# Expert weights in 2 MB blocks with 16 KB rows, buffered in eight blocks of four slots, and another order of expert units

## The chip, the cores and the metric

The kernel runs on one core of one Trainium2 chip. Its engines are TensorE (PE, with its weight loads shown as PEld), VectorE (DVE), ScalarE (ACT), GpSimd (POOL) and SyncE (SP), whose queue issues nearly all loads from HBM. Each engine takes its own instructions in order and waits on semaphores for the others. The metric is the device time of one execution in microseconds, the median of several runs. All data are 32-bit floats.

## What is computed

Two layers over 256 latent tokens and 256 context tokens of width 1024. A layer modulates and normalises its input, mixes it with three head groups (a chunked gating MLP, a 2-D Fourier mixing, a windowed attention), projects, and applies a channel mixer. The channel mixer of layer 0 is dense; that of layer 1 sends each of the 256 latent tokens to two of eight experts of inner width 3584:

```python
logits = (y @ w_r).astype(jnp.float32) + b_r.astype(jnp.float32)
top_val, top_idx = lax.top_k(logits, TOP_K)
gates = jax.nn.softmax(top_val, axis=-1)
combine = jnp.sum(jax.nn.one_hot(top_idx, N_EXPERTS, dtype=jnp.float32) * gates[..., None], axis=-2)
for e in range(N_EXPERTS):
    out = out + combine[..., e:e + 1] * ((jax.nn.silu(y @ wg[e]) * (y @ wu[e])) @ wd[e])
```

Gate, up and down matrices of the eight experts are 352 MB together; every one of them is read once, whatever the routing.

## The kernel before

**An order written out beforehand.** The program is built by a planner (`Sched`, L91 on). Work is written as Python generators, called tasks; each step of a task names an engine, the buffers it needs and the events it waits for. The planner keeps a virtual clock for each engine, charges each instruction a cost (`Eng.cost`, L239; `DM` for a load of 512 KB in the expert stage), and always takes the step that could start first, with a bias per task. What comes out is one fixed instruction order for each engine. A buffer that a task takes in the plan becomes, on the chip, a wait for the readers of whatever was in it before.

**Buffers.** SBUF holds 41 slots of [128, 1024] floats (512 KB each, pool "s", `slot` L292), and smaller ones ("h", "q"). `get` (L133) gives out the slot that has been free longest. A load takes a slot in the class "raw"; `sc.rest` is the number of slots that loads must leave to all other uses (`avail`, L111). In the expert stage it is 8, from step 7 of the list below 17, and from step 28 again 8 (`REST`, L53): loads can fill 33, 24 and 33 slots.

**The expert stage.** `experts` (L1488) works through units. Unit None is expert 0, whose address is known from the start, with 32 token slots. Units 0 to 6 are the other seven experts by falling number of tokens, with 160, 96, 96, 64, 64, 64 and 32 token slots (`SLOTS`); SP reads their numbers into registers once the routing tables are made (`t_comb`, L1251, spawned with the bias `CB`; it ends with the table of overflowing tokens). What exceeds the slots of a unit is done in extra rounds under a branch (`moe_over`, L1646). `SEQ` (L68) lists the order as (unit, first block, last block): inner width 3584 is seven blocks of 512 columns, and one block of one unit is a step, 56 steps in all. Each entry of `SEQ` ends with a down product over its blocks and a finish (`t_finish`, `t_xfinish`), which spreads the result over the tokens and adds it up.

A step needs a gate, an up and a down piece of 2 MB, each loaded as four DMAs of 512 KB whose rows are 4 KB (`moe_items` L1674, `t_load` L378). The load order is gate and up of step n, then down of step n-1. Parts of 128 token slots (only unit 0 has one, beside a part of 32) use weights split into a high and a low half, made by ScalarE and VectorE (`t_hi` L401, `t_lo` L409), and three matmuls a product (`t_egu`, `t_edown`). Parts of 64 and 32 slots (`t_xgu` L1551, `t_xdown` L1592) read the loaded pieces as they are. `raw_done` (L418) and `done` (L423) free a slot after its last use, each 512 KB for itself. Within an entry of `SEQ` the gate and up tasks of all steps are spawned before the down task, so that in the plan they come first when both could run.

Of the kernel before, what the change touches and what calls it, by code (L numbers as in the profile page):

```python
# [24 lines left out]
D = 1024  # L25
KC = 8
NE = 8
# [32 lines left out]
LAT = (0.26, 0.2)  # L60
DF, DM = 0.4, 1.27
SGB, FOB, PRB = (-0.3, -0.3), (-0.3, -0.5), (-0.5, 0.0)
# [4 lines left out]

SEQ = ((None, 0, 7), (0, 0, 2), (3, 0, 7), (0, 2, 4), (4, 0, 7), (0, 4, 7), (5, 0, 7), (1, 0, 7), (2, 0, 7), (6, 0, 7))  # L68

# [21 lines left out]
class Sched:  # L91
# [3 lines left out]
    def __init__(self, make):  # L95
        self.make = make
        self.clock = {e: 0.0 for e in (PE, ACT, DVE, POOL, DMA, NONE)}
        self.live, self.cur, self.num = [], None, 0
        self.free, self.cap, self.held, self.own = {}, {}, {}, {}
        self.rest = 0  # L100

# [9 lines left out]
    def avail(self, res):  # L111

        need, cls_need = {}, {}
        for r in res:
            p, _, c = self.parse(r)
            need[p] = need.get(p, 0) + 1
            cls_need[p, c] = cls_need.get((p, c), 0) + 1
        t = 0.0
        for p, n in need.items():
            if len(self.free[p]) < n:  # L120
                return None
            t = max(t, self.free[p][n - 1][0])
        for (p, c), n in cls_need.items():
            if (p, c) in self.cap and self.held.get((p, c), 0) + n > self.cap[p, c]:
                return None
            if c == "raw" and len(self.free[p]) - n < self.rest - self.others():
                return None
        return t

    def others(self):  # L130
        return sum(n for (p, c), n in self.held.items() if p == "s" and c != "raw")

    def get(self, res):  # L133
        out = []
        for r in res:
            p, dt, c = self.parse(r)
            _, tag = self.free[p].pop(0)
# [44 lines left out]
    def step(self, t):  # L182
        self.live.remove(t)
        self.cur = t
        eng, res, _ = t.req
        if res:
            t.ready = max(t.ready, self.avail(res))
        try:
# [97 lines left out]
class Core:  # L286
# [5 lines left out]
    def slot(self, tag, dt=F32):  # L292
        return self.sb.tile([128, 1024], dt, tag=tag, name=tag)

# [83 lines left out]
    def t_load(self, items):  # L378
        for kind, key, ap in items:
            if kind == "rest":  # L380
                self.sc.rest = ap
                self.sc.cap["s", "raw"] = 40 if ap else 6
# [7 lines left out]
            if callable(ap):  # L390
                if self.uidx is None:
                    yield on(DMA, ev=[self.combed])
                    self.uidx = [self.nc.values_load(self.unum[0:1, r:r + 1], engines=(mybir.EngineType.SP,),
                                                     min_val=0, max_val=NE - 1) for r in range(NE - 1)]
                ap = ap()
            raw = yield on(DMA, "s:raw")
            self.nc.sync.dma_start(raw, ap)
            self.sc.charge(DMA, self.dcost)
            self.sc.set(self.raw[key], raw, 1.9)

    def t_hi(self, items):  # L401
        for kind, key, ap in items:
            if kind not in ("w", "wn"):
# [14 lines left out]
    def raw_done(self, key):  # L418
        self.ruses[key] -= 1
        if self.ruses[key] == 0:  # L420
            self.sc.rel(self.raw[key].v)

    def done(self, key):  # L423

        self.uses[key] -= 1
        if self.uses[key] == 0:
            self.sc.rel(*self.piece[key].v)

    def stream(self, items):

        items = [it if len(it) == 4 else (*it, 1) for it in items]
        for kind, key, ap, n in items:
            self.raw[key], self.piece[key], self.uses[key] = Event(), Event(), n
            self.ruses[key] = len(kind)
# [1053 lines left out]
    def experts(self, units, seq):  # L1488
# [3 lines left out]
        for key, b0, b1 in seq:  # L1492
# [27 lines left out]
            near = [hts[max(b0, b1 - 2)]]  # L1520
            if (key, b0, b1) == seq[-1] and key < NE:
# [124 lines left out]
    def moe_over(self):  # L1646

        tc, nc = self.tc, self.nc
        novf = nc.values_load(self.onum[0:1, MORE:MORE + 1], min_val=0, max_val=MORE)
        oidx = [nc.values_load(self.onum[0:1, i:i + 1], engines=(mybir.EngineType.SP,), min_val=0, max_val=NE - 1)  # L1650
# [23 lines left out]
    def moe_items(self, seq, idx=None):  # L1674
# [3 lines left out]

        def piece(name, e, *at):
            if idx is None and e == 0:  # L1680
                return a[name][(e, *at)]

            def by_register():
                i = self.uidx[e - 1] if idx is None else idx
                return a[name][(bass.ds(i, 1), *at)].rearrange("o p f -> (o p) f")

            return by_register

        kind = lambda e: "".join(dict.fromkeys("n" if ws else "w" for _, ws in self.parts(self.slots(e)))) if idx is None else "w"
        it = []  # L1690
        for n in range(len(steps) + 1):
            if n < len(steps):
                e, b = steps[n]
                if idx is None:
                    it += [("rest", None, r) for m, r in REST[1] if n == m]
                for k, name in (("eg", "w_gate_e"), ("eu", "w_up_e")):
                    it += [(kind(e), (k, e, b, j), piece(name, e, b, j)) for j in range(4)]
            if n > 0:
                e, b = steps[n - 1]
                it += [(kind(e), ("ed", e, b, j), piece("w_down_e", e, 4 * b + j)) for j in range(4)]  # L1700
        return it
# [42 lines left out]
    def build(self):  # L1744
        with self.tc.tile_pool(name="sb", bufs=1) as sb, \
                self.tc.tile_pool(name="ps", bufs=1, space=bass.MemoryType.PSUM) as psp:
            self.sb, self.psp = sb, psp
            with self.tc.manual_schedule():
                self.body()

    def body(self):
        nc, a = self.nc, self.a
        sc = self.sc = Sched({"s": self.slot, "h": self.half, "q": self.quarter, "b": self.bank, "p": lambda tag, dt: tag})
        sc.pool("b", [f"b{i}" for i in range(8)])
        sc.pool("s", [f"s{i}" for i in range(NS)])
        sc.pool("h", [f"f{i}" for i in range(NH)])
# [7 lines left out]
        R2, R8 = range(2), range(8)  # L1764
        self.raw, self.piece, self.uses, self.ruses, self.uidx = {}, {}, {}, {}, None
        self.gate, self.colev = ev(R2, (2, 5), R2), ev(R2, (0, 1, 3, 4, 5))
# [5 lines left out]
        self.hT = [Event() for _ in range(7)]  # L1772
        self.dcost = DM
        self.cev_h, self.lev_h, self.lev_c = [[Event() for _ in range(FC)] for _ in range(3)]
# [178 lines left out]
def _layout(i):  # L1953
# [51 lines left out]
```

## Time and profile before

| | us |
|---|---|
| median of 3 runs | 1710.16 (1707.85 to 1710.85) |
| the profiled execution, its own time | 1710.48 |
| its span, first to last instruction | 1708.6 |
| PE busy | 1635.1 (96%) |
| VectorE busy | 778.1 (46%) |
| ScalarE busy | 536.1 (31%) |
| moved by DMA | 497.78 MB, mean 291 GB/s |

The profile comes from one execution. Busy time is time with an instruction under way; PE's matmuls are pipelined and their ends are modelled. A matmul of plain 32-bit floats is two records, one on split halves is one. The granted clock is given as a share of full speed; its mean was 0.985. "Idle before" is the time in which the engine had nothing under way ahead of an instruction, with what ended it. Nearly all compute instructions carry line 232, the helper that records them, so groups are told apart by their shapes: `128*64 128x512` is a matmul with a stationary operand of 128x64 and an output of 512 columns.

### The profile page before, as it was taken

What the parts mean: (1) busy time and instruction counts of PE and PEld (TensorE: products, weight loads), DVE (VectorE), ACT (ScalarE), POOL (GpSimd) and SP (SyncE); (2) the same over time, 40 slices, a digit from 0 to 9 for tenths busy, and PEclk for the clock granted to TensorE, in tenths of its full rate; (3) what the DMA queues carried; (4) which work ended last, traced back from release to release, by engine and by line L of the source; (5) the groups of instructions that cost most, each with busy time, mean ns of one, the idle gap of its engine ahead of it and who ended that gap; (6) DMA issues with size and microseconds to landing.
All of it is one profiled execution on the core that took longest, in us unless ns stands there. A gap on an engine that the chain in (4) does not pass through costs nothing. (4 is left out here: it accounts for less than half of the span.)

```text
span 1708.6 us, 33100 instructions
## 1 busy us (share of the span) xinstructions
PE 1635.1 (96%) x13308; PEld 1146.5 (67%) x13308; DVE 778.1 (46%) x1426; ACT 536.1 (31%) x945; POOL 26.1 (2%) x49
## 2 busy tenths in 40 slices
PE   6999999999999999998987999999999999999995
PEld 3776889888888888886664754755675565466452
DVE  4576688765644458887506521620752110020022
ACT  3476453322222235556414312410531000000011
POOL 0100000000000010000000000000000000000000
PEclk9999999999999999999899999999999999999997
DMA  9515436544544455773699899999999999999995
GB/s 370 203 38 235 161 136 215 180 164 144 193 153 159 172 203 200 284 264 130 246 367 392 329 414 413 400 409 414 412 352 413 413 412 412 414 412 397 391 411 228
DMA packets 137890, 497.78 MB, mean 291 GB/s; under 512 B 16349, under 2 KB 16481, under 8 KB 137729
## 3 DMA queue, kind: packets, MB, share of 16 engines
q1 hardware_dynamic: 135072, 490.79, 74.9%
q0 software_dynamic: 1792, 4.18, 0.8%
q8 instruction: 106, 1.74, 0.4%
q10 hardware_dynamic: 864, 0.62, 0.1%
q14 instruction: 56, 0.45, 0.1%
HBM read 494.49 MB, written 1.05 MB: 290 GB/s over the span
## 5 line engine op out<-in xcount | busy, mean ns | idle before, releaser
L232 PE MATMUL b<-s,s 128*128 128x512 f32 (+3 forms) x6056 | 873.4, 344 | 18.7 <-DVE s L232 16.6
L232 PEld LDWEIGHTS b<-s,s 128*128 128x128 f32 (+2 forms) x6056 | 663.2, 157 | 192.2 <-issue 40.5
L232 PE MATMUL b<-s,f 128*32 128x128 f32 (+5 forms) x5472 | 520.6, 355 | 29.2 <-DVE ones L632 8.6
L232 PEld LDWEIGHTS b<-s,f 128*32 128x32 f32 (+2 forms) x5472 | 319.2, 129 | 206.1 <-issue 92.8
L232 DVE TENSOR_TENSOR s<-s,s 128x1024 fp32r<-128x1024 f32 (+2 forms) x253 | 303.1, 1216 | 70.4 <-ACT s L232 60.3
L232 ACT ACTIVATE s<-s 128x1024 fp32r<-128x1024 f32 (+1 forms) x257 | 265.4, 1052 | 180.5 <-PE b L232 94.2
L232 DVE TENSOR_TENSOR f<-f,b 128x256 f32<-128x256 f32 (+3 forms) x91 | 39.0, 430 | 469.5 <-PE b L232 469.3
L232 ACT ACTIVATE f<-b 128x512 f32<-128x512 f32 (+4 forms) x161 | 77.6, 483 | 425.8 <-PE b L232 424.8
L232 PE MATMUL b<-s,q 128*64 128x512 f32 (+2 forms) x752 | 161.0, 587 | 6.0 <-issue 4.5
L232 DVE SCALAR_TENSOR_TENSOR s<-s,cs,s 128x1024 f32<-128x1024 f32 x73 | 91.8, 1279 | 40.1 <-DMA s<-in_w_ada_dram 39.8
L232 ACT ACTIVATE q<-b 128x128 f32<-128x128 f32 (+2 forms) x53 | 18.0, 341 | 256.1 <-PE b L232 256.1
L232 PEld LDWEIGHTS b<-s,q 128*64 128x64 f32 (+2 forms) x752 | 47.5, 132 | 74.3 <-issue 53.4
L232 DVE TENSOR_TENSOR s<-b,s 128x512 fp32r<-128x512 f32 (+2 forms) x85 | 53.8, 638 | 80.0 <-ACT s L232 57.3
L232 ACT ACTIVATE s<-b 128x512 fp32r<-128x512 f32 (+3 forms) x107 | 54.6, 533 | 86.5 <-PE b L232 75.3
L232 PE MATMUL b<-ident,f 128*128 128x128 f32 x313 | 56.5, 290 | 7.0 <-DVE smx L232 3.1
L232 PEld LDWEIGHTS b<-ident,f 128*128 128x128 f32 x313 | 35.0, 143 | 41.8 <-DVE f L232 22.4
L232 DVE SCALAR_TENSOR_TENSOR s<-b,utab,s 128x512 f32<-128x512 f32 x56 | 40.8, 748 | 42.1 <-PE b L232 42.0
L232 ACT ACTIVATE f<-f 128x256 fp32r<-128x256 f32 x28 | 11.7, 419 | 114.9 <-DVE f L232 114.9
L232 PEld LDWEIGHTS b<-q,h 128*128 128x128 f32 x288 | 35.6, 200 | 5.7 <-issue 2.4
L232 DVE TENSOR_TENSOR f<-b,f 128x512 fp32r<-128x512 f32 x5 | 3.4, 689 | 78.5 <-ACT f L232 78.5
L232 PE MATMUL b<-q,h 128*128 128x32 f32 (+3 forms) x288 | 36.9, 284 | 0.8 <-DVE q L232 0.8
L232 ACT ACTIVATE f<-b,cols 128x256 f32<-128x256 f32 (+1 forms) x56 | 25.9, 555 | 34.4 <-PE b L232 31.3
(154 smaller groups left out, 565.9 us busy)
## 6 DMA issues: line engine op xcount, KB each, us to landing
s<-in_w_gate_e_dram SPq DMA_DIRECT2D x224, 512.0 KB, 10.0
s<-in_w_up_e_dram SPq DMA_DIRECT2D x224, 512.0 KB, 10.0
s<-in_w_down_e_dram SPq DMA_DIRECT2D x224, 512.0 KB, 10.0
s<-in_w_ada_dram SPq DMA_DIRECT2D x96, 512.0 KB, 4.5
s<-in_w_down_d_dram SPq DMA_DIRECT2D x56, 512.0 KB, 4.3
s<-in_w_gate_d_dram SPq DMA_DIRECT2D x28, 512.0 KB, 4.3
s<-in_w_up_d_dram SPq DMA_DIRECT2D x28, 512.0 KB, 3.4
s<-in_w_in_dram SPq DMA_DIRECT2D x24, 512.0 KB, 7.5
```

Source lines behind the costliest of these rows:

```text
L232: r = f(out, *a, **k)
```

## The change

The arrays of the expert weights are laid out so that one gate, up or down piece of a step is 128 rows of 16 KB, and one DMA loads all 2 MB. For that the last 32 of the 41 slots are made as eight small pools of four ("low"); the first nine (`KEEP`) stay single. `block` gives up such a pool and forms one tile of [128, 4096] in its place ("high", pool "Q") as soon as its four slots are free and a load asks for it. Until step 6 a load may also take four single slots, as four DMAs of 512 KB; then only blocks. From step 7 to 28, loads leave three blocks to the split halves, which now live in blocks too, two pieces in each. A block is freed when all four pieces in it are used. Single slots are no longer given out oldest first: among those free for 4 us (`SLACK`), the first nine go first, and then those of the group with the fewest free. The planner's cost of an expert load falls from 1.27 to 1.22 for 512 KB, the bias of the routing tables from 12.5 to 3.0, unit 6 is cut in two around unit 2, and the parts of a step are spawned in reverse, the 32-slot part of unit 0 first. Before the overflow rounds, all remaining groups become blocks.

```diff
-CB = 12.532
+CB = 3.0
-REST = (8, ((7, 17), (28, 8)))
+REST = (0, ((6, 9, 0), (7, 9, 3), (28, 9, 0)))
+KEEP, SLACK, NEAR = 9, 4.0, 2
-DF, DM = 0.4, 1.27
+DP, DF, DM = 1.27, 0.4, 1.22
-SEQ = (..., (5, 0, 7), (1, 0, 7), (2, 0, 7), (6, 0, 7))
+SEQ = (..., (5, 0, 7), (1, 0, 7), (6, 0, 4), (2, 0, 7), (6, 4, 7))
...
+    def block(self):
+        q = self.free["Q"]
+        ok = lambda: len(q) - 1 >= self.qrest - self.held.get(("Q", "hl"), 0) and len(q) > 0
+        more = lambda: len(self.free["s"]) - 4 >= self.rest - self.others()
+        have = {tag: t for t, tag in self.free["s"]}
+        four = lambda i: all(tag in have for tag in range(i, i + 4))
+        when = lambda tags: max(have[tag] for tag in tags)
+        while not ok() and self.low and more() and four(i := KEEP + 4 * self.low - 4):
+            self.free["s"] = [x for x in self.free["s"] if not i <= x[1] < i + 4]
+            self.low -= 1
+            q.append((when(range(i, i + 4)), self.low))
+            self.convert()
+        solo = None
+        if self.solo and more() and len(self.free["s"]) > 3:
...
+            solo = when(tags), tags
+        return q[0][0] if ok() else None, solo
...
+    def convert(self):
+        self.low.pop().release()
+        n = len(self.low)
+        self.high[n] = self.tc.alloc_tile_pool(name=f"high{n}", bufs=1, side="right", reuse_waits="tile")
...
+            if kind[0] == "b":
...
+                t = yield on(DMA, "B:raw")
+                cols = lambda x, j: x[:, j * 1024:j * 1024 + 1024]
+                if isinstance(t, list):
+                    for j in range(4):
...
+                        self.nc.sync.dma_start(t[j], cols(ap, j))
...
+                else:
+                    own = [t, 4 * len(kind) - 4]
+                    self.nc.sync.dma_start(t, ap)
+                    self.sc.charge(DMA, 4 * self.dcost)
+                    for j in range(4):
+                        self.rown[(*key, j)] = own
+                        self.sc.set(self.raw[(*key, j)], cols(t, j), 1.9)
...
+            if kind in ("bw", "bwn", "bnw"):
+                for j in range(4):
+                    k0 = (*key, j)
+                    if j % 2 == 0:
+                        t = yield on(ACT, "Qr:hl", ev=[self.raw[k0]])
+                        own = [t, 2]
...
     def raw_done(self, key):
-        self.ruses[key] -= 1
-        if self.ruses[key] == 0:
-            self.sc.rel(self.raw[key].v)
+        own = self.rown[key]
+        own[1] -= 1
+        if own[1] == 0:
+            self.sc.rel(own[0])
...
             for b in range(b0, b1):
-                for s, ws in parts:
+                for s, ws in reversed(parts):
...
-        o[n] = i[n].reshape(NE, 4, 2, 128, EB, 512).transpose(0, 4, 1, 3, 2, 5).reshape(NE, EB, 4, 128, 1024)
-    o["w_down_e"] = i["w_down_e"].reshape(NE, FC, 128, D)
+        o[n] = i[n].reshape(NE, 4, 2, 128, EB, 512).transpose(0, 4, 3, 1, 2, 5).reshape(NE, EB, 128, 4096)
+    o["w_down_e"] = i["w_down_e"].reshape(NE, EB, 4, 128, D).transpose(0, 1, 3, 2, 4).reshape(NE, EB, 128, 4096)
```

## Rows read from the trace of the kernel before

**Rows 1.** Page, 40 slices of the span: PE's busy tenths and the DMA rate

```profile
PE   6999999999999999998987999999999999999995
...
GB/s 370 203 38 235 161 136 215 180 164 144 193 153 159 172 203 200 284 264 130 246 367 392 329 414 413 400 409 414 412 352 413 413 412 412 414 412 397 391 411 228
```

**Rows 2.** DMA issues: destination<-source, engine, count, KB each, median us to landing

```profile
s<-in_w_gate_e_dram SPq DMA_DIRECT2D x224, 512.0 KB, 10.0
```

**Rows 3.** Windows: us, busy us (records) of PE, PEld, DVE, ACT, POOL; clock, DMA share, GB/s

```profile
859.20:912.00 52.80, 43.77 (x949) 29.60 (x939) 9.37 (x61) 8.64 (x22) 1.84 (x2) 0.97 1.02 405
912.00:1000.00 88.00, 80.41 (x670) 55.46 (x668) 51.39 (x87) 33.74 (x48) 0.00 (x0) 0.96 0.94 361
1000.00:1240.00 240.00, 239.46 (x1942) 142.72 (x1940) 84.88 (x103) 66.51 (x94) 0.00 (x0) 1.00 1.02 410
1240.00:1280.00 40.00, 40.00 (x311) 28.97 (x311) 21.62 (x27) 15.88 (x21) 0.00 (x0) 1.00 0.95 348
1280.00:1560.00 280.00, 279.62 (x3261) 160.19 (x3265) 35.92 (x66) 22.74 (x49) 0.00 (x0) 1.00 1.03 412
1560.00:1600.00 40.00, 40.00 (x531) 23.70 (x523) 3.64 (x11) 2.84 (x6) 0.00 (x0) 1.00 0.99 376
1600.00:1687.00 87.00, 78.31 (x1163) 38.36 (x1156) 9.65 (x18) 6.76 (x19) 0.00 (x0) 0.96 1.02 409
1640.00:1691.00 51.00, 41.69 (x626) 20.20 (x615) 1.44 (x5) 3.75 (x12) 0.00 (x0) 0.93 0.94 379
```

**Rows 4.** Timeline of SP's queue: start us, duration us, issues merged

```profile
842.34 16.72 SPq L397 DMA_DIRECT2D s<-in_w_down_e_dram  x4
859.17 1.98 SPq L397 DMA_DIRECT2D s<-in_w_gate_e_dram  x4
```

**Rows 5.** The output stores in the issue table, and the window of their transfer

```profile
out_dram<-s SPq DMA_DIRECT2D x4, 256.0 KB, 2.0
...
1704.80:1706.80 2.00, 0.00 (x0) 0.00 (x0) 0.84 (x2) 0.00 (x0) 0.00 (x0) 0.50 1.02 393
```

**Rows 6.** PE by shape, 1400 to 1453 us: count, busy us, mean ns, idle before

```profile
L232 PE MATMUL b<-s,s 128*64 128x256 f32 x230 | 27.1, 382 | 0.4 <-DMA s<-in_w_gate_e_dram 0.4
L232 PE MATMUL b<-s,s 128*32 128x128 f32 x464 | 14.3, 274 | 0.0
```

**Rows 7.** PE by shape, 1592.6 to 1628.3 us

```profile
L232 PE MATMUL b<-s,f 128*64 128x512 f32 x88 | 20.6, 601 | 0.0
L232 PE MATMUL b<-s,f 128*32 128x512 f32 x96 | 11.5, 596 | 0.0
```

**Rows 8.** PE by shape, 930 to 1690 us: the three-product matmuls

```profile
L232 PE MATMUL b<-s,s 128*128 128x512 f32 x492 | 123.8, 401 | 0.1
```

**Rows 9.** PE by shape, 1640 to 1691 us

```profile
L232 PE MATMUL b<-s,q 128*32 128x512 f32 x112 | 22.1, 628 | 1.9 <-issue 0.8 <-DMA s<-in_w_down_e_dram 0.5 <-SPq L1654 0.4
L232 PE MATMUL b<-s,f 128*32 128x128 f32 x493 | 18.4, 282 | 5.7 <-DMA s<-in_w_up_e_dram 3.9 <-DMA s<-in_w_gate_e_dram 1.5 <-issue 0.3
```

**Rows 10.** Timeline of PE where the 160 unit begins

```profile
917.80 0.50 PE L232 MATMUL b<-s,s 128*128 128x512 f32 x1 [2.95 <-DVE s L232]
922.94 4.24 PE L232 MATMUL b<-s,s 128*128 128x512 f32 x10 [4.64 <-DVE s L232]
```

**Rows 11.** Timeline of VectorE there: the overflow table's first row, the first splits

```profile
907.92 0.16 DVE L232 TENSOR_SCALAR f<-rank 128x7 f32<-128x7 f32 x1
...
916.52 5.77 DVE L232 TENSOR_TENSOR s<-s,s 128x1024 fp32r<-128x1024 f32 x5
```

**Rows 12.** Timeline of ScalarE there: splits that waited for the first gate pieces

```profile
912.04 2.22 ACT L232 ACTIVATE s<-s 128x1024 fp32r<-128x1024 f32 x2 [2.69 <-DMA s<-in_w_gate_e_dram]
...
915.77 1.06 ACT L232 ACTIVATE s<-s 128x1024 fp32r<-128x1024 f32 x1 [0.27 <-DMA s<-in_w_gate_e_dram]
```

**Rows 13.** Timeline of PE: the last finish

```profile
1694.46 3.64 PE L232 MATMUL b<-s,q 128*128 128x512 f32 x8 [3.70 <-issue]
```

More of the change, by code (lines that the diff above doesn't have):

```diff
@@ L111, in avail @@
     def avail(self, res):
+        if res[0] == "B:raw":
+            tq, ts = self.block()
+            return min((t for t in (tq, ts and ts[0]) if t is not None), default=None)
         need, cls_need = {}, {}
@@ L131, in others @@
         return sum(n for (p, c), n in self.held.items() if p == "s" and c != "raw")
-    def get(self, res):
-        out = []
-        for r in res:
-            p, dt, c = self.parse(r)
-            _, tag = self.free[p].pop(0)
+    def block(self):
[12 more added lines that the diff above has]
+        if self.solo and more() and len(self.free["s"]) > 3:
+            fours = [range(i, i + 4) for i in (0, 4, *range(KEEP, KEEP + 4 * self.low, 4)) if four(i)]
+            tags = min(fours, key=lambda f: (when(f), -f[0])) if fours else [tag for _, tag in self.free["s"][:4]]
+            solo = when(tags), tags
+        return q[0][0] if ok() else None, solo
@@ new lines, in settle, with group @@
+    def settle(self, rest, qrest):
+        self.rest, self.qrest, self.solo = rest, qrest, False
+        while self.low:
+            self.low -= 1
+            i = KEEP + 4 * self.low
+            t = max(t for t, tag in self.free["s"] if i <= tag < i + 4)
+            self.free["s"] = [x for x in self.free["s"] if not i <= x[1] < i + 4]
+            self.free["Q"].append((t, self.low))
+            self.convert()
+    def group(self, tag):
+        return -1 if tag < KEEP else (tag - KEEP) // 4
@@ new lines, in get @@
+    def get(self, res):
+        out, at = [], None
+        if res[0] == "B:raw":
+            tq, ts = self.block()
+            if ts is None or tq is not None and tq <= max(ts[0], self.now):
+                res = ["Q:raw"]
+            else:
+                res, at = ["s:raw"] * 4, ts[1]
+        for i, r in enumerate(res):
+            p, dt, c = self.parse(r)
+            free = self.free[p]
+            if p == "s":
+                if at is not None:
+                    x = next(x for x in free if x[1] == at[i])
+                else:
+                    room = {}
+                    for _, tag in free:
+                        room[self.group(tag)] = room.get(self.group(tag), 0) + 1
+                    old = [x for x in free if x[0] <= self.now - SLACK] or free[:1]
+                    x = min(old, key=lambda x: (x[1] >= KEEP, room[self.group(x[1])], x[1]))
+                free.remove(x)
+                tag = x[1]
+            else:
+                _, tag = free.pop(0)
@@ L187, in step @@
             t.ready = max(t.ready, self.avail(res))
+        self.now = max(t.ready, self.clock[eng])
         try:
@@ L402, in t_hi @@
         for kind, key, ap in items:
[L403 removed]
+            if kind in ("bw", "bwn", "bnw"):
[4 more added lines that the diff above has]
+                        own = [t, 2]
+                    else:
+                        yield on(ACT, ev=[self.raw[k0]])
+                    h, l = [t[:, o:o + 1024] for o in (j % 2 * 2048, j % 2 * 2048 + 1024)]
+                    raw = self.raw[k0].v
+                    self.s.activation(h, raw, AF.Copy)
+                    self.pown[k0] = own
+                    self.sc.spawn(self.t_lo(k0, raw, h, l, self.sc.cur.ready), self.sc.cur.bias)
+                continue
+            if kind != "w":
                 continue
@@ L1747, in build @@
             self.sb, self.psp = sb, psp
+            self.low = [self.tc.alloc_tile_pool(name=f"low{i}", bufs=1, reuse_waits="tile") for i in range((NS - KEEP) // 4)]
+            self.high = {}
             with self.tc.manual_schedule():
                 self.body()
+            for p in [*reversed(self.high.values()), *reversed(self.low)]:
+                p.release()
     def body(self):
         nc, a = self.nc, self.a
-        sc = self.sc = Sched({"s": self.slot, "h": self.half, "q": self.quarter, "b": self.bank, "p": lambda tag, dt: tag})
+        sc = self.sc = Sched({"s": self.slot, "Q": self.quad, "h": self.half, "q": self.quarter, "b": self.bank, "p": lambda tag, dt: tag})
         sc.pool("b", [f"b{i}" for i in range(8)])
-        sc.pool("s", [f"s{i}" for i in range(NS)])
+        sc.pool("s", range(NS))
+        sc.pool("Q", [])
+        sc.low, sc.convert = len(self.low), self.convert
         sc.pool("h", [f"f{i}" for i in range(NH)])
```

72 lines of the change are left out of this document (47 added, 25 removed).

## The prediction

> **What bounds the kernel now.** I read the 40 slices first [rows 1]. From slice 25 to the end PE stands at 9 and the DMA moves some 410 GB/s: the expert stage, about 850 us, looks bound by both. The issue table says what the transfers are: 224 loads of 512 KB for each of the three expert matrices, 10 us from issue to landing, so about eight are under way at a time [rows 2] (the row of the gate stands for three alike). The windows by stage part the two [rows 3]. 412 GB/s is the rate at which nothing disturbs the DMA (1280 to 1560 us), 512 KB in 1.272 us. It falls to 361 (912 to 1000), 348 (1240 to 1280) and 376 (1560 to 1600): the DMA waits there for free slots, because PE is behind. PE, on the other hand, is idle for 0.5 us of 240 and 0.4 of 280. It is idle in two places only: 7.6 us of 88 after 912, and 9.3 us of the 51 from 1640 to 1691. So the DMA sets the pace at both ends of the stage, and PE between.
>
> The sum of the DMA: SP's queue sat full from 842 until a slot came free, and went on from 859.2 [rows 4]. 41 slots were full then, so 631 of 672 loads were left, 631 x 1.272 = 803 us. They kept their rate until about 1687, 828 us later: 25 us were waiting for slots. Behind the last landing stand the last down product, to 1690.8, and 18 us of finish and output.
>
> **The change, part by part.**
>
> *Rate.* The same bytes come with a quarter of the DMAs and rows four times as long. No row shows 16 KB rows. Two row lengths are shown: 4 KB at 412 GB/s [rows 3], and the four output stores with 2 KB rows at 393 GB/s [rows 5]. One of 16 DMA engines thus takes 4096 x 16 / 412 = 159.1 ns for a 4 KB row and 83.4 ns for a 2 KB row: 75.7 ns per 2 KB and 7.7 ns for each row. A 16 KB row comes to 8 x 75.7 + 7.7 = 613 ns, which is 428 GB/s, 4.9 us for 2 MB or 1.226 us per 512 KB. It is an estimate: the stores go the other way. Bounds: no gain at all (1.272), and the overhead gone altogether (1.211). I take 1.226. For 631 loads the DMA then needs 774 us, 29 less. An expert step (gate, up, down) costs it 14.7 us in place of 15.3.
>
> The Trainium skill, "DMA: Bandwidth & Descriptors", speaks in its section "Why small descriptors are slow (HBM only)" of a fixed overhead for each packet, and in "SWDGE vs HWDGE vs iDMA" of packets of preferably at most 4096 B. The 7.7 ns agree with there being an overhead. If a 16 KB row were still cut into 4 KB packets, nothing of it would be saved, and the sum would be that of the rival "the rate stays".
>
> *What PE needs.* The prices of one step, from rows at full clock. 64 slots: 64 records of 256 columns at 0.118 [rows 6] and 16 of 512 at 0.234 [rows 7], with two transposes 11.7 us. 32 slots: 128 records at 0.031 and 16 at 0.12, 6.2 us. 96 is the sum, 17.6. 160 has 72 records at 0.25 [rows 8] beside a part of 32, 24 us. From the first step of the 160 unit on: 7 x 24 + 14 x 17.6 + 21 x 11.7 + 7 x 6.2 = 703 us, and the gathers and finishes of the units. The trace says the same from the other side: the 779 us from 912 to 1691, less 7.6 and the 17 worked out below, are 754 us of PE's work, so some 51 of gathers and finishes. The DMA needs 49 x 15.3 = 750 for these steps now and 49 x 14.7 = 720 afterwards. With the faster rate PE is the bound of everything after 912, and of 29 us only that part can be had in which PE now waits.
>
> *How much that is.* End of the stage: from 1640 to 1691 PE ran 493 records of 128 columns and 112 of 512 [rows 9]. At the dense prices of [rows 6, 7] that is 15 to 18 and 13.4, with the few others some 34 us of work in 51. 17 us are data arriving late: idle time, and runs cut into groups of 16 and less. With PE behind the DMA to the end, they go.
> Start: PE waits 2.95 + 4.64 us for the first splits of the 160 unit [rows 10], since VectorE is with the overflow table from 907.9 to 916.5 and only then splits [rows 11]. Bias 3.0 in place of 12.5 for that table brings it forward into VectorE's idle time (busy 9.4 us of 52.8 before 912 [rows 3]), and the reversed parts put the 32-slot part, which needs no split, first. Against this, a block is usable only when all of it has landed (3.7 us after its first quarter now [rows 12]), and the first block comes free when four quarters are used, about 1.5 us after the first. The first gate block of this unit lands at about 859.2 + 1.5 + 44 x 1.226 + 2 = 917, where PE now begins in earnest at 920 to 923. I take 4 us gained; bounds 0 and 7.6.
> Added: unit 6 is cut in two, one more finish: 8 matmuls, as the last one in 3.6 us [rows 13]; 4 us. Its ScalarE and VectorE work lies beside PE's.
> The other tags of the single slots and the pools' change-over: before 739 us the loads have slack; 0 (bounds -2 and +4).
>
> *What is late next: the lead.* The DMA runs ahead of PE by what the buffers hold. Now it is 33 slots, or 24 while 17 are reserved: 42 or 30 us. Afterwards it is 8 blocks, or 5 beside 3 for the splits, and of these one is always partly used: 7 x 4.9 = 34 us, or 4 x 4.9 and six split pieces, 27. SP is in order: a load that waits for a block holds all later loads; PE is too, and a wait for a block holds the finishes behind it. Heavy units fill the lead, light ones drain it. A 64-slot unit drains 7 x (14.7 - 11.7) = 21 us of 27 or 34. Unit 6's first four steps drain 4 x 8.5 = 34 us of 34, its last three 26 of 34. A 96-slot unit fills 7 x 2.9 and its gather and finish, about 30. So PE should just not starve. The first four steps of unit 6 have no margin; for them, and for blocks that land late, I allow 4 us.
>
> *Sum.* 1708.6 - 17 - 4 + 4 + 4 = 1695.6 us of span. The profiled execution took 1710.48 us, 1.9 more than its span, and the median is 0.3 below that: 1697 us. The bounds of these terms give 1691 to 1702.
>
> **The rivals.**
>
> *All of the DMA's gain arrives.* If PE's busy time contains waiting, the DMA alone is the bound: 1710 - 29 + 3 for blocks that are usable later = 1684. For it: weight loads are busy only 160 of 280 us where PE shows 279.6 [rows 3]. Against it: the records run at one price in every stretch, and where data is late, gaps do show [rows 9, 10]. "Trainium Kernel Development and Optimization" of the Trainium skill, section "Performance Expectations", calls matmul busy time a bad measure of how close a kernel is to its limit, and the busy share of weight loads a good one; by that rule it would come out like this.
>
> *The rate stays* at 412 GB/s, because the cost is per 4 KB and not per row. Then the DMA needs 803 us again and stays the last: the earlier table and the order of units give some 4 us, the coarser blocks take some back: 1708 (1702 to 1714). For it: no 16 KB row is in the trace. Against it: the 2 KB rows did pay more.
>
> *The blocks are too coarse: slower.* One mechanism: a 2 MB block comes free only when its last quarter is used, and PE takes down products late; of the 36 us from 1592.6, 32 are down products, 88 and 96 records at 16 a step, so that some 22 loads of one unit were held [rows 7]. That would be five or six of eight blocks. If it takes one and a half blocks (7.4 us) from the lead, PE starves by about that at four places, at the end of the two 64-slot units between the 160 stretches and in both pieces of unit 6: 4 x 7.4, less the 4 allowed, 25.6 us on top: 1722 us. It costs more than the change brings from 17 us of starving in all, 4.3 at each place, which is less than one block. For it: the margins above are small. Against it: PE can take its downs earlier.
>
> *Blocks come together late:* loads go on as four singles where no group of four is free. That costs only rate, and only until step 6, from which on every load is a block. It is inside the range.
>
> **How the numbers follow.** PE-bound as worked out, 1691 to 1702: 0.55. All of the DMA's gain (1680 to 1690): 0.10. The rate stays (1702 to 1714): 0.17, of which 0.05 lie under 1706.7. Too coarse (1714 to 1733): 0.18. The range from 1685 to 1717 holds about 8 in 10; the forecast's own is 1691 to 1702. 0.2% is 3.4 us, about what can be told from no change: faster 0.55 + 0.10 + 0.05 = 0.70, same 0.12, slower 0.18.
>
> **What would show it.** Right: some 56 loads of 2048 KB for each matrix in the issue table; stretches of some 428 GB/s where the DMA is not held; deeper dips than now in the stretches of the 160 and 96 units, while PE stays full; no wait of 4 us for VectorE at the first split; PE's last steps without gaps of 0.6 us for the DMA. Wrong: 412 GB/s again; or waits of PE of 3 us and more for gate and up blocks in unit 6 and at the end of the 64-slot units, the third rival; or falling prices of PE's records, the first.

## The result and the profile after

The changed kernel takes 1690.88 us (median of 4 runs, 1688.31 to 1693.2) against 1709.01 (1705.56 to 1710.85): a ratio of 0.9896 [0.9873, 0.9919]. The prediction was 1697 us, faster: a gain of 13 us forecast, 18 measured. Its time came nearly right, but by a sum in which several terms were wrong and cancelled; the experiments below show which. One run of experiment e2 took 2035.62 us at a granted clock of 0.75 and is left out of its median.

The page of the kernel after: busy time by engine, PE's busy tenths, the DMA rate, the packets, and the issue table (answers to [rows 1, 2]).

```profile
PE 1618.4 (96%) x13316; PEld 1155.1 (68%) x13316; DVE 780.8 (46%) x1432; ACT 534.7 (32%) x947; POOL 26.2 (2%) x49
...
PE   6999999999999999999979999999999999999996
...
GB/s 374 205 38 237 164 136 205 182 170 153 176 160 164 172 191 202 323 240 135 261 289 423 380 427 425 383 420 427 397 306 422 427 425 425 424 407 424 425 425 198
DMA packets 71779, 497.64 MB, mean 294 GB/s; under 512 B 9004, under 2 KB 9136, under 8 KB 52048
...
w<-in_w_down_e_dram SPq DMA_DIRECT2D x52, 2048.0 KB, 18.2
w<-in_w_up_e_dram SPq DMA_DIRECT2D x51, 2048.0 KB, 18.6
w<-in_w_gate_e_dram SPq DMA_DIRECT2D x50, 2048.0 KB, 17.8
```

153 of the 168 pieces came as 2 MB blocks, and where nothing holds the DMA it moves 425 to 427 GB/s. The packets tell the rows: 71779 - 52048 = 19731 are of 8 KB and more, and 153 blocks have 153 x 128 = 19584 rows. A 16 KB row is one packet.

The windows of the kernel after, with the columns of [rows 3]; the last one ends with PE's last down product.

```profile
859.20:912.00 52.80, 41.56 (x724) 32.25 (x720) 15.79 (x88) 10.11 (x24) 0.95 (x1) 0.86 0.90 355
912.00:1000.00 88.00, 87.51 (x781) 58.98 (x775) 47.06 (x59) 32.06 (x45) 0.00 (x0) 1.00 0.97 402
1000.00:1240.00 240.00, 235.75 (x1930) 145.22 (x1924) 88.94 (x105) 73.10 (x103) 0.00 (x0) 1.00 0.95 397
1240.00:1280.00 40.00, 39.48 (x283) 26.94 (x283) 17.43 (x28) 8.36 (x14) 0.00 (x0) 1.00 0.98 389
1280.00:1560.00 280.00, 273.78 (x3363) 161.51 (x3361) 37.55 (x76) 21.93 (x51) 0.00 (x0) 1.00 1.00 422
...
1640.00:1673.00 33.00, 31.80 (x503) 17.12 (x499) 8.48 (x14) 4.43 (x11) 0.00 (x0) 1.00 0.80 339
```

Against [rows 3] three things have moved. The start is worse: 355 GB/s for 405 before 912 us. The stretch after it is better: PE lost 0.5 us of 88 there, 7.6 before. And PE, which had hardly a gap from 1000 to 1560, now loses 4.25 + 0.52 + 6.22 us there, while the end is dense: 1.2 us lost of 33 for 9.3 of 51. From 1640 to 1691 us PE's records of 512 columns with 32 slots are dense again too: 48 of this form took 5.6 us, where 112 took 22.1 [rows 9].

```profile
L292 PE MATMUL b<-w,q 128*32 128x512 f32 x48 | 5.6, 596 | 0.2 <-SPq L1770 0.2
```

The timeline of PE in the kernel after, from the first gather of the expert stage to the first run of the 160 unit (answers to [rows 10]).

```profile
839.32 5.70 PE L292 MATMUL b<-q,h 128*128 128x32 f32 x32 [0.81 <-DVE q L292]
...
856.45 1.25 PE L292 MATMUL b<-s,f 128*32 128x128 f32 x34 [2.54 <-issue]
...
869.29 2.05 PE L292 MATMUL b<-s,f 128*32 128x128 f32 x67 [2.88 <-issue]
...
890.20 3.64 PE L292 MATMUL b<-w,f 128*32 128x128 f32 x64 [5.67 <-DMA w<-in_w_up_e_dram]
...
917.77 4.44 PE L292 MATMUL b<-w,s 128*128 128x512 f32 x18
```

Before, the gather stood at 849.83 and the dense run began at 922.94 [rows 10]. It is 10.5 us earlier now, and of these only 5.2 are left when the 160 unit begins, at 917.77. The waits for VectorE are gone: its timeline shows the overflow table from 877.59 to 886, and the splits in one run as soon as ScalarE has done its half (answers to [rows 11]).

```profile
877.59 0.16 DVE L292 TENSOR_SCALAR f<-rank 128x7 f32<-128x7 f32 x1
...
915.93 9.31 DVE L292 TENSOR_TENSOR w<-w,w 128x1024 fp32r<-128x1024 f32 x8 [2.07 <-ACT w L292]
```

### The profile page after: what moved, and what is told of

The parts are those of the page before. It is cut to its first block, busy times and chain, and to the rows that moved or that the text cites. A ratio compares the mean times of both kernels' runs of the same rounds, so it can differ in the third digit from the quotient of the medians.

```text
span 1691.4 us, 31271 instructions
## 1 busy us (share of the span) xinstructions
PE 1618.4 (96%) x13316; PEld 1155.1 (68%) x13316; DVE 780.8 (46%) x1432; ACT 534.7 (32%) x947; POOL 26.2 (2%) x49
## 2 busy tenths in 40 slices
DMA packets 71779, 497.64 MB, mean 294 GB/s; under 512 B 9004, under 2 KB 9136, under 8 KB 52048
## 5 line engine op out<-in xcount | busy, mean ns | idle before, releaser
L292 PE MATMUL b<-s,s 128*128 128x512 f32 (+2 forms) x2864 | 580.6, 364 | 7.9 <-DVE s L292 6.8
L292 PEld LDWEIGHTS b<-s,s 128*128 128x128 f32 (+1 forms) x2864 | 460.7, 187 | 96.1 <-issue 10.0
L292 PE MATMUL b<-w,f 128*32 128x128 f32 (+3 forms) x3776 | 304.9, 356 | 11.6 <-DMA w<-in_w_up_e_dram 7.0
L292 PE MATMUL b<-w,s 128*32 128x128 f32 (+2 forms) x3192 | 282.0, 324 | 4.3 <-DMA w<-in_w_gate_e_dram 4.3
L292 PEld LDWEIGHTS b<-w,s 128*32 128x32 f32 (+2 forms) x3192 | 204.1, 130 | 80.9 <-issue 28.2
L292 PEld LDWEIGHTS b<-w,f 128*32 128x32 f32 (+1 forms) x3776 | 170.4, 122 | 130.1 <-issue 85.3
L292 PE MATMUL b<-s,f 128*32 128x128 f32 (+2 forms) x1696 | 210.4, 359 | 22.2 <-DVE ones L747 8.6
L292 ACT ACTIVATE s<-s 128x1024 fp32r<-128x1024 f32 (+2 forms) x173 | 179.0, 1050 | 145.3 <-PE b L292 84.1
L292 PEld LDWEIGHTS b<-s,f 128*32 128x32 f32 (+1 forms) x1696 | 155.2, 146 | 64.8 <-issue 13.3
L292 PE MATMUL b<-w,q 128*64 128x512 f32 (+1 forms) x608 | 112.3, 597 | 2.1 <-DMA w<-in_w_down_e_dram 1.9
```

Source lines behind the costliest of these rows:

```text
L292: r = f(out, *a, **k)
```

## How the runs are compared

One number stands for the DMA's waiting. Each kernel's window from 860 to 1640 us has a mean rate, and the window from 1420 to 1460 shows its rate where nothing is held. **Held** time is 780 us x (1 - mean / undisturbed): the load time lost while SP stood before slots or blocks that were still in use. A load that is held is landed later, and so is everything behind it: by the packet records of the traces, the last packet of the expert weights lands at 1688.4 us before, 1674.6 in e10, 1670.4 in e4, 1688.7 in e1 and 1670.6 after, and each span ends 20 to 21 us later. The rates are whole GB/s, and one GB/s is 1.9 us in 780; the loads of 512 KB into single slots show 411 to 414 GB/s where nothing holds them, from one profile to the next. So held times are good to some 4 us. The two rows of each kernel, first the kernel before:

```profile
860.00:1640.00 780.00, 762.45 (x8170) 458.53 (x8166) 215.03 (x366) 153.18 (x246) 1.84 (x2) 0.99 1.01 400
...
1420.00:1460.00 40.00, 40.00 (x508) 24.15 (x509) 4.61 (x13) 2.46 (x5) 0.00 (x0) 1.00 1.03 412
```

The kernel after:

```profile
860.00:1640.00 780.00, 755.55 (x8082) 467.54 (x8076) 209.55 (x359) 149.97 (x245) 0.95 (x1) 0.99 0.98 406
...
1420.00:1460.00 40.00, 40.00 (x544) 25.27 (x536) 3.08 (x10) 2.84 (x6) 0.00 (x0) 1.00 1.01 427
```

| kernel | median us | first gather | dense run of the 160 unit | GB/s undisturbed | held us |
|---|---|---|---|---|---|
| before | 1709.0 | 849.8 | 922.9 | 412 | 22.7 |
| before, early table and reversed parts (e10) | 1698.1 | 847.0 | 914.6 | 414 | 13.2 |
| before, all but the blocks (e4) | 1692.7 | 845.0 | 912.8 | 414 | 11.3 |
| after, 4 KB rows (e1) | 1713.5 | 838.5 | 912.8 | 408 | 22.9 |
| after, 8 KB rows (e3) | 1695.6 | 838.2 | 912.3 | 418 | 24.3 |
| after | 1690.9 | 839.3 | 917.8 | 427 | 38.4 |

The bytes are nearly the same in all: some 631 loads of 512 KB after about 860 us, 331 MB, which is 799 us at 414 GB/s, 811 at 408 and 775 at 427.

## The experiments

**Rows, DMAs and blocks, with the plan of the kernel after.** The first three keep every engine's order.

e1, four DMAs for a block:

```diff
-                    self.nc.sync.dma_start(t, ap)
+                    for j in range(4):
+                        self.nc.sync.dma_start(cols(t, j), cols(ap, j))
```

> The kernel after, but each 2 MB block is filled by four DMAs of 512 KB with 4 KB rows; the order of all engines is that of after. Theory (the time of a transfer is 7.7 ns for each row and 75.7 ns for 2 KB, whatever the DMA's size): undisturbed windows fall from 427 to 412 GB/s, the DMA needs 29 us more for the expert stage, some of which its waits for free blocks take up; about 1700 us (1696 to 1710). Rival 'the cost is per DMA': 412 GB/s as well, the same time; the next kernel parts them. Rival 'the rate has nothing to do with the time, only the order has': 1689 to 1693 us, even with 412 GB/s.

e2, one DMA of 2 MB from the arrays of the kernel before, so that its rows are 4 KB:

```diff
-                    self.nc.sync.dma_start(t, ap)
+                    self.nc.sync.dma_start(t.rearrange("p (j f) -> p j f", j=4), ap)
...
-        o[n] = i[n].reshape(NE, 4, 2, 128, EB, 512).transpose(0, 4, 3, 1, 2, 5).reshape(NE, EB, 128, 4096)
+        o[n] = i[n].reshape(NE, 4, 2, 128, EB, 512).transpose(0, 4, 1, 3, 2, 5).reshape(NE, EB, 4, 128, 1024)
```

> The kernel after with one DMA of 2 MB for a block, but the arrays in HBM as before, so that its rows are 4 KB; the order is that of after. Theory (per row): 412 GB/s, and the time of the kernel with four DMAs of 512 KB within 3 us, about 1700 us. Rival 'the cost is per DMA': 427 GB/s and 1691 us.

e3, two DMAs of 1 MB:

```diff
-                    self.nc.sync.dma_start(t, ap)
+                    for j in (0, 2):
+                        self.nc.sync.dma_start(t[:, j * 1024:j * 1024 + 2048], ap[:, j * 1024:j * 1024 + 2048])
```

> The kernel after with two DMAs of 1 MB with 8 KB rows for a block. Theory (per row): 4 x 75.7 + 7.7 = 310.5 ns for 8 KB, 422 GB/s, and some 3 us above after at most: 1691 to 1695 us. Rival 'a row above 4 KB pays nothing more, the gain is from the count of DMAs': between 412 and 427 as well, about 420; with the second kernel at 412 this rival falls.

The windows of e1:

```profile
860.00:1640.00 780.00, 755.20 (x7924) 450.06 (x7917) 211.57 (x359) 151.95 (x242) 0.95 (x1) 0.99 1.01 396
...
1420.00:1460.00 40.00, 39.23 (x508) 23.80 (x512) 3.08 (x10) 2.35 (x5) 0.00 (x0) 1.00 1.03 408
```

and of e2, the second window alone:

```profile
1420.00:1460.00 40.00, 38.46 (x554) 24.30 (x550) 2.47 (x7) 2.45 (x5) 0.00 (x0) 1.00 1.03 408
```

and of e3:

```profile
860.00:1640.00 780.00, 757.52 (x8060) 458.88 (x8056) 210.30 (x359) 151.47 (x245) 0.95 (x1) 0.99 0.99 405
...
1420.00:1460.00 40.00, 38.98 (x548) 24.67 (x544) 3.62 (x11) 2.35 (x5) 0.00 (x0) 1.00 1.01 418
```

e1 took 1713.49 us, 1.004 [1.0025, 1.0055] of the kernel before; e2 1714.5, 1.0036 [1.0019, 1.0053]; e3 1695.55, 0.9935 [0.9914, 0.9955]. Four DMAs of 512 KB and one of 2 MB move the same 408 GB/s when their rows are 4 KB, so the rival of a cost per DMA has fallen: the row counts. One of 16 DMA engines needs 160.6 ns for 4 KB, 313.6 for 8 KB, 613.9 for 16 KB; taken two at a time they leave 7.6, 9.5 and 13.3 ns for the row itself, 7.7 was the estimate, and 613 the estimate for 16 KB; e3's 418 is a little under its expected 422. The time follows, but not in step: 427 to 418 GB/s is 17 us more of transfer and costs 4.7 us, 418 to 408 is 19 us more and costs 17.9. And e1, which has all of the change but the long rows, is slower than the kernel before. That was not expected: 1696 to 1710 was. The rival that only the order counts has fallen with it.

**The plan without the blocks.** e4 is the kernel before with the early table, the new order of units, the reversed parts, and loads that take their four slots together in the plan; the slots stay single, loaded by 512 KB and freed one by one. It lacks the blocks, and what serves them: the new way of giving out single slots, the planner's lower cost and the numbers of reserved blocks. The part that is not a constant:

```diff
+            if key[0] in ("eg", "eu", "ed"):
+                if key[3] == 0:
+                    four = yield on(DMA, "F:raw")
+                else:
+                    yield on(DMA)
+                raw = four[key[3]]
+            else:
+                raw = yield on(DMA, "s:raw")
```

> The kernel before (loads of 512 KB with 4 KB rows into single slots) with the rest of the change: a block's four slots taken together in the plan, the bias 3.0, the new order of units, the reversed parts. Theory (the 10.5 us before the expert stage come from the plan, which puts the attention of layer 1 in another order once loads take slots in fours; what comes after needs the rate): first gather at about 839 to 843 us in place of 850, 412 GB/s, the end of the stage bound by the DMA again, 1698 to 1706 us. Rival 'it is the plan alone': 1691 us. Rival 'the rate is all of it, and the earlier gather is won back by waiting': 1707 to 1711 us.

It took 1692.68 us, 0.9912 [0.9895, 0.9928]: the first rival, not the theory; the first gather, at 844.97 us, is later than the theory had it. With 4 KB rows and 414 GB/s it cannot be told from the kernel after. Its windows:

```profile
860.00:1640.00 780.00, 768.77 (x8199) 461.94 (x8203) 211.83 (x361) 152.21 (x248) 1.84 (x2) 0.99 1.02 408
...
1420.00:1460.00 40.00, 40.00 (x513) 23.37 (x505) 3.64 (x11) 2.85 (x6) 0.00 (x0) 1.00 1.03 414
```

Held time has halved, from 22.7 to 11.3 us, and the first gather is 4.9 us earlier: 16.3 us, and the kernel is 15.7 faster. That the two come so close is partly chance: 414 GB/s for 412 would be another 4 us, and the first gather has a spread of its own (846.5 to 849.8 us in before, e6 and e9, whose instruction order up to there is the same). From e4 to e1 the blocks come in at 4 KB rows: 11.6 us more held, 12 us more for 331 MB at 408 in place of 414 GB/s, 23.6 together; measured 20.8. From e1 to after the rows grow: 36 us less transfer, 15.5 more held, 20.5 together; measured 22.6. So the change is three parts: **the plan -15.7, the blocks and what serves them +20.8, the rows -22.6 us** (by the ratios to the kernel before -15.0, +21.9 and -24.6; each is good to some 4 us). They are taken in this order, the plan first; longer rows without the new plan weren't run, so what the rows would have gained there is open. The other way of giving out slots lies in the second part, but its earlier gather is gone by the time the 160 unit runs, at 912.8 us in both kernels. Why 4 KB rows go at 411 to 414 GB/s into single slots and at 408 into blocks isn't settled; the arrays are not the reason, since e2 has the old ones.

**The parts of the plan, each alone in the kernel before.**

e5 takes the four slots together and changes nothing else (the diff above).

> The kernel before; in the plan alone, an expert load takes its four slots together; loads stay 512 KB, all constants are those of before. Theory (the plan's taking of fours is what puts the attention of layer 1 in another order and brings the expert stage forward): first gather at 839 to 845 us in place of 850, then the stage of before with its waits for the splits and the DMA held at the same places: 1701 to 1706 us. Rival (the stage begins when its data is there, not when the gather is): 1707 to 1711 us.

e6 changes the order of units:

```diff
-(5, 0, 7), (1, 0, 7), (2, 0, 7), (6, 0, 7))
+(5, 0, 7), (1, 0, 7), (6, 0, 4), (2, 0, 7), (6, 4, 7))
```

> The kernel before with the new order of units alone (unit 6 cut in two around unit 2). Theory (before, the DMA is held for slots from 1540 to 1620 us, 396 and 389 GB/s for 412, some 4 us, and then has to feed unit 6 alone; with a light piece ahead of unit 2 it is not held there): 1702 to 1706 us, and no stretch under 405 GB/s after 1500. Rival (the cut brings a finish and nothing else): 1709 to 1713 us.

e10 has the early table and the reversed parts:

```diff
-CB = 12.532
+CB = 3.0
...
-                for s, ws in parts:
+                for s, ws in reversed(parts):
```

> The kernel before with the early tables (bias 3.0) and the reversed parts alone. Theory (the two waits for VectorE's splits, 7.6 us, go, PE takes the first blocks of the 160 unit sooner, and the DMA is held less in 912 to 1000, 361 GB/s before; since the DMA is the bound at the end, what it is held less comes off the end): 4 to 7 us less, 1702 to 1706 us. Rival (PE only stands in front of its next limit): 1707 to 1711 us.

e5 took 1704.39 us, 0.9976 [0.9962, 0.999]; e6 1707.93, 0.9991 [0.998, 1.0001]; e10 1698.07, 0.9934 [0.9908, 0.996]. e5 is where its theory had it, e6 between its theory and its rival, and e10 below its theory: 11.8 us by the medians, 11.3 by the ratio, with an interval of 6.8 to 15.7. By the ratios the three parts alone come to -16.9, and e4, which has all three, to -15.0. Two things change together in e10, the bias and the order of the parts; which of them counts wasn't parted. The windows of e10:

```profile
912.00:1000.00 88.00, 88.00 (x745) 57.60 (x737) 47.09 (x59) 31.57 (x45) 0.00 (x0) 1.00 1.02 408
...
860.00:1640.00 780.00, 769.07 (x8342) 465.42 (x8334) 214.81 (x366) 152.43 (x249) 1.84 (x2) 1.00 1.02 407
...
1420.00:1460.00 40.00, 40.00 (x553) 24.37 (x545) 5.16 (x13) 3.11 (x7) 0.00 (x0) 1.00 1.03 414
```

While PE waited for the splits it freed no slots, and the DMA ran at 361 GB/s from 912 to 1000 [rows 3]; now it runs at 408. Held time falls by 9.5 us, and 88 x (1 - 361/412) - 88 x (1 - 408/414) = 9.6 us of it lie in this window. The gather is 2.9 us earlier too, but that is within the spread of before, e6 and e9, and the order up to there is theirs. In e6 and e9 the two waits for the splits, which this change removes, took 9.7 and 9.5 us, in the profile before 7.6 [rows 10]. The two of e6:

```profile
916.76 0.79 PE L232 MATMUL b<-s,s 128*128 128x512 f32 x1 [5.38 <-DVE s L232]
921.90 4.63 PE L232 MATMUL b<-s,s 128*128 128x512 f32 x10 [4.35 <-DVE s L232]
```

So the waits are paid, as far as can be told in full; that they cost more than themselves can't be told from the noise. In e6 the stretch from 1540 to 1620 is no longer held (410 GB/s), but the time did not move enough to be told from nothing. In e5 the attention of layer 1 begins earlier: its first mask product stands at 773.43 us, 787.45 before. The gather came at 843.17, and then the old waits for the splits, as the timelines of PE show, first the kernel before, then e5:

```profile
787.45 0.23 PE L232 MATMUL b<-maskb,identb 128*128 128x128 bf16 x1
```

```profile
773.43 0.23 PE L236 MATMUL b<-maskb,identb 128*128 128x128 bf16 x1
...
911.92 0.49 PE L236 MATMUL b<-s,s 128*128 128x512 f32 x1 [3.95 <-DVE s L236]
917.07 3.97 PE L236 MATMUL b<-s,s 128*128 128x512 f32 x10 [4.65 <-DVE s L236]
```

**More work for PE.** 56 matmuls that nobody needs, the same edit in both kernels:

```diff
+                if key == 6 and b < 4:
+                    go(self.t_warm(14, [hts[b]]))
```

> The kernel after with 56 needless bf16 matmuls of 512 columns, 14 behind each of the first four steps of unit 6, some 12 us more of work for PE at full clock. Theory (PE sets the pace of the kernel after): 1699 to 1704 us. Rival (data sets the pace, and the work fills waits): 1690 to 1695 us.

> The kernel before with the same 56 needless matmuls as the after of the run before it, 14 behind each of the first four steps of unit 6, some 12 us of PE's time. Theory (unit 6 is the end of the kernel before, and there the data sets the pace: 17 us of waiting in 51): most of it falls in waits, 0 to 4 us more than before, 1709 to 1714 us. Rival (PE is the bound there too): 12 us more, 1719 to 1724 us.

Both expectations name the wrong place: `key` counts expert 0 too, so key 6 is unit 5 of the order, with 64 slots. The timeline of PE in e8 shows the first 14, followed by the next instruction,

```profile
1283.08 3.20 PE L292 MATMUL b<-identb 128*128 128x512 bf16 x14
1285.93 0.82 PE L292 MATMUL b<-s,q 128*128 128x512 f32 x2
```

2.85 us this time and 3.1 each of the three others, 12.2 in all. e8 took 1703.51 us, 0.9959 [0.9947, 0.997], which is 12.6 more than after (10.8 by the two ratios); e9 1719.7, ratio 1.0061 [1.0041, 1.0082], 9.9 more than before (7 to 14 by the interval), the rival of its expectation. So e9 says nothing of unit 6. It says something else: in the middle of the kernel before PE has no gap, the extra work is paid, in full as far as can be told, and although PE waits for data at the end, that waiting does not take it up. The windows show why, first the kernel before, then e9:

```profile
1500.00:1540.00 40.00, 40.00 (x609) 25.69 (x613) 7.30 (x11) 2.94 (x6) 0.00 (x0) 1.00 1.03 412
1540.00:1620.00 80.00, 80.00 (x1046) 44.03 (x1038) 4.19 (x12) 4.31 (x9) 0.00 (x0) 1.00 1.01 392
```

```profile
1500.00:1540.00 40.00, 40.00 (x491) 21.89 (x489) 8.82 (x13) 3.26 (x6) 0.00 (x0) 1.00 0.87 322
1540.00:1620.00 80.00, 80.00 (x1140) 48.13 (x1140) 4.75 (x13) 5.67 (x12) 0.00 (x0) 1.00 0.99 377
```

Against the kernel before, that is 40 x (1 - 322/412) + 80 x (15/412) = 11.6 us of loads held, and the end, which waits for the last of them, moves along.

**Towards a better version.** e7 makes pairs of the blocks (1 MB, 8 KB rows, freed by two pieces), e11 has one pair more, e12 reserves two blocks for the halves in place of three. e7 and e11 also reserve six pairs for the halves and have 1.25 for the planner's cost. The remarks behind # say which kernel a line is of.

```diff
-REST = (0, ((6, 9, 0), (7, 9, 3), (28, 9, 0)))
+REST = (0, ((6, 9, 0), (7, 9, 2), (28, 9, 0)))   # e12
+KEEP, SLACK, NEAR, G = 9, 4.0, 2, 2              # e7; e11: KEEP 7
+                for j0 in range(0, 4, G):
+                    t = yield on(DMA, "B:raw")
...
+                        self.nc.sync.dma_start(t, cols(ap, j0, G))
```

> The kernel after with sixteen blocks of two slots in place of eight of four: a DMA brings 1 MB in 8 KB rows, and a block comes free when two pieces are used. Theory (at equal rate, coarse blocks cost the stage some 18 us, as the after with 4 KB rows stands to the plan without blocks, and 16 KB rows give them back): about 418 GB/s, half the cost of the blocks gone, PE less idle in the 96 and 64 units, 1681 to 1688 us, faster than both kernels. Rival (PE is the bound at 427 GB/s and does not mind the blocks): 1689 to 1694 us.

> The kernel with pairs (1 MB in 8 KB rows), with seven single slots in place of nine, so that there are seventeen pairs. Theory (the lead of the DMA is what is short): one pair more in flight is 2.5 us of lead, the DMA held less at 1060, 1220 and 940 us, 1690 to 1701 us against 1704.7 with sixteen. Rival (the pairs lose by the plan's other order at the start of the 160 unit, where the clock was granted at 0.86 and the DMA at 323 GB/s): 1701 to 1707 us.

> The kernel after with two blocks kept for the split halves in place of three, from step 7 to 28. Theory (PE's 14 us of idle in 912 to 1672 are the short lead of the blocks; one more block for loads is 4.9 us of lead while the 160 unit runs): 1 to 5 us less, 1686 to 1690 us. Rival (with two blocks the splits of the next operand wait for the last use of the one before, and PE for them): PE waits for ACT and DVE in the 160 stretches, 1695 to 1715 us.

e7 took 1704.7 us, 0.9964 [0.9949, 0.998]; e11 1702.49, 0.9957 [0.9939, 0.9974]; e12 1689.42, 0.9877 [0.9845, 0.9909]. e7 misses both its theory and its rival by 10 us and more, and e11 is in the range of its rival. The pairs move 418 GB/s as e3 does; e7 is 9.1 us slower than e3 by the medians and 5.0 by the ratios, whose intervals overlap, and 37.3 us of loads are held (398 of 418) where e3 has 24.3. The two windows of e7, and a third that shows a part of it:

```profile
860.00:1640.00 780.00, 753.77 (x7885) 454.39 (x7877) 209.84 (x353) 149.79 (x241) 0.00 (x0) 0.99 0.98 398
...
1420.00:1460.00 40.00, 39.58 (x519) 24.34 (x509) 3.42 (x11) 2.45 (x5) 0.00 (x0) 1.00 1.01 418
...
900.00:940.00 40.00, 37.18 (x429) 25.43 (x430) 20.65 (x21) 18.77 (x24) 0.00 (x0) 0.86 0.87 323
```

The list of waits for the third window says that SP stood there 13.3 us for VectorE's splits and 17.7 for PE; e3 has 412 GB/s in it. What finer blocks do at one and the same order of work was thus not measured. e12 falls within its expectation, but its interval overlaps that of the kernel after: no version here is shown to beat it.

## Why the prediction came near, and by what it was wrong

**Read from the two profiles alone, the sum fits.** The 160 unit begins 5.2 us earlier, where the prediction had 4. From there to the end of the last down product it is 767.8 us before and 755.3 after, 12.5 less, where the terms -17, +4 and +4 make -9. What follows is 0.5 us longer. The last down products, before and after:

```profile
1688.85 1.90 PE L232 MATMUL b<-s,q 128*32 128x512 f32 x10 [0.18 <-SPq L1654]
```

```profile
1671.12 1.92 PE L292 MATMUL b<-w,q 128*32 128x512 f32 x16 [0.20 <-SPq L1770]
```

**Taken apart, it doesn't.** The prediction gave 17 less 4, 13 us, to the rows and blocks, and nothing to the plan, whose -4, +4 and 0 cancel. Run one after the other, the blocks and rows came to -1.8 us and the plan to -15.7. The plan brings nearly the same time without any long row. That the time came near is in this respect luck.

**The rate: right.** 428 GB/s was predicted, 427 came, and e1 to e3 bear out the reason given, a cost for each row. By the Trainium skill, "DMA: Bandwidth & Descriptors", section "SWDGE vs HWDGE vs iDMA", a packet is preferably at most 4096 B, which is said there of what GpSimd's descriptors make, while these loads are issued by SP; the packets counted in the profile show 16 KB rows unsplit, and they are the faster ones. The section "Measured (HBM→SBUF, 128 partitions, SWDGE, issued from GpSimd)" of the same page of the Trainium skill has the rule to batch DMAs to 1 MiB and more for at least 75% of the peak; by it the 2 MB of e2 should have been ahead of the 512 KB of e1, and with several under way both moved 408 GB/s.

**PE as the bound of the kernel after: right in the main.** From 8 KB to 16 KB rows the transfer is 17 us shorter, and the kernel only 4.7: there the rate no longer sets the pace. PE was busy for 745.6 of the 760 us from 912 to 1672, and 12.2 us of work cost 10.8 to 12.6; but this alone doesn't part the kernels, since it cost the kernel before as much. 14 us of waits are left, 10.6 of them for blocks.

**The first rival, that busy time contains waiting, has a grain of truth.** PE's busy time fell by 16.7 us, from 1635.1 to 1618.4, with eight matmul records more. So up to 17 us that were shown as busy before were waiting: the 112 records that came late took 0.197 us each, the 48 dense ones 0.117, since a record with nothing close behind it counts with its whole length (628 ns in the mean). The prediction reckoned with this for the last 51 us only. The line of the kernel before:

```profile
PE 1635.1 (96%) x13308; PEld 1146.5 (67%) x13308; DVE 778.1 (46%) x1426; ACT 536.1 (31%) x945; POOL 26.1 (2%) x49
```

Dense records keep the prices of [rows 6], 0.116 to 0.118 us for 256 columns and 64 slots, and the 1684 us of the rival did not come.

**"For blocks that land late, I allow 4 us": the term furthest off.** e1 is 20.8 us slower than e4, with 4 KB rows in both. By the sums above about half of that is the lower rate into blocks (408 GB/s for 414), a cost that the prediction did not have at all, and the other half is held time, which doubles with blocks that come free only when four pieces are used. The rival "too coarse" had a like size, 25.6, but by starving alone. PE's gaps appear in the middle of the stage, in the windows of 1000 to 1560 of the profile after; from 912 to 1672 PE waited 12 times for gate blocks, at most 1.5 us each and 7.4 us together, not 4.3 and more at four places. The rival lost because the longer rows pay its cost back.

**"Start ... I take 4 us gained": too small for the plan by itself.** In the kernel after the 160 unit begins at 917.77 us; the prediction had the first gate block landing at 917. In the kernel before without blocks, the early table and the reversed parts bring 11.3 us (6.8 to 15.7). The wait was priced against the landing of the first block; what it also does is hold loads (9.6 us in that window). The prediction read the 25 us of waiting for slots as a thing of the DMA's own and looked for PE's gain only where PE waits. e10 and e9 show that while the buffers are full a delay of PE delays the DMA, and the end of the kernel pays for it.

**"The other tags ... 0 (bounds -2 and +4)": wrong side.** The gather came 10.5 us earlier, or 7 against the earliest gather of the old order. Two pieces can be told apart. Loads that take four slots let the attention of layer 1 start earlier; e5 has the gather at 843.2, where the four profiles without it have 846.5 to 849.8. And SP's load of the Fourier matrices stands at 723.12 us in the kernel after, 721.9 to 725.2 in the seven others with the new giving-out of slots, and 728 to 730 in the six without; this policy wasn't run alone. About half of the 10.5 us is lost again before the 160 unit, while the DMA moves only 319 GB/s from 840 to 900 us and PE waits 5.67 us for one block.

**The end, -17, and the finish, +4.** The gaps of the end are gone, as predicted. As a term it can't be read off alone: e10 and e4 gain 12 and 16 us and still wait there, 7.5 and 3.3 us of the 33 from 1640 to 1673. The finish isn't seen: the order alone is -1.9 us, no difference that can be told.

**Two of its sums are off**, without weight for the outcome: 11.7 and 6.2 make 17.9 us for a step of 96 slots, not 17.6, which is 4 us in 14 steps; and the upper bounds that it names (nothing gained at the start, +4 for the tags) lead to 1705, not 1702.

**The rival "the rate stays"**, 1702 to 1714 us, was run as e1 and e2: 1713.5 and 1714.5, the upper end. The plan's gain and the cost of the blocks nearly cancel there, which the prediction had as "4 us" and "some back".

## What to carry to other kernels

Where a stream of loads fills all buffers, a wait of the consuming engine is paid at the end, even if the end seems to be bound by the loads: look at the loads that it holds (mean against undisturbed rate) and not only at who waits last. Into the same blocks, rows of 16 KB gave nearly 5% more rate than rows of 4 KB, but the blocks and what serves them cost nearly as much as that was worth, and most of the gain was there at 8 KB. A change made of several parts is best taken apart before it is believed: here the plan alone, with the early table and the reversed parts above all, brought what the whole change brought.

## What was not expected of the hardware

One 16 KB row travelled as one packet, at 614 ns in one of the 16 DMA engines against 642 for four rows of 4 KB, both worked out from the rates (427 and 408 GB/s). At 4 KB rows, one DMA of 2 MB was no faster than four of 512 KB.
